# Attention scores: maximum pass that also copies to SBUF, whole-row exponentials, a one-pass difference, and 512-column projection products

## Chip, cores and metric

One core of a Trainium2 chip runs the whole program in one launch. The metric is device time in microseconds (us); the kernel before takes 5096.02 us, the median of 3 runs (5091.18 to 5097.48).

## What is computed

Two layers act on 2048 latent rows and 256 context rows of width 1024, all in float32. Layer one is an RWKV-7 mixer (input projection, two scans, readout and output product). Layer two, which the change is mostly about, is differential attention: 8 heads, each with two 64-wide query/key components and a 128-wide value.

```python
proj = h @ w_in                                   # q, k, v, g, 1024 columns each
s = jnp.einsum("bqhcd,bkhcd->bchqk", q_blk, k_all).astype(jnp.float32) * scale
p = jax.nn.softmax(s, axis=-1)                    # over 2304 keys, for c = 0 and 1
attn = p[:, 0] - lam * p[:, 1]
o = jnp.einsum("bhqk,bkhe->bqhe", attn, v_all)
y = rms_norm(o, subln) * (1.0 - lam_init)
x = x + gate * ((y * jax.nn.silu(g)) @ w_out)
```

## The kernel before

The stages follow each other: `phase1` (projection of layer one, from 0 to 1140 us in the profile), `phase2` (scans, to 2270), `readout` (to 2612), `project1` (layer two's projection, to 3398), `attention` (to 4870) and `finish` (output product). Float32 products are made of three products of split operands: a high part (float32r) and the rest, `matmul_split`, L928 to L933.

`readout` multiplies 18 blocks of 128 rows with the layer's output weights, four quarters of 256 columns each, and does norms on VectorE, ScalarE and GpSimd beside it; the string READ (L936) sets the order. `project1` goes over two groups of 1152 rows and eight chunks of 512 columns; each chunk's weights come as two tiles of 256 columns (`in_weights`, L1133), and a block of 128 rows takes 2 x 8 x 3 products of 256 columns (L1264 to L1266). The weights of the next chunk are asked for a third and two thirds of the way through a chunk (L1259).

`attention` goes over 8 heads with 16 query tiles of 128 rows each, 128 steps and two more that drain. The string STEP (L1294) sets one order for every engine, and `in_order` (L47) pins it on TensorE, VectorE, ScalarE and GpSimd: nothing overtakes. Step n does these for different tiles:

- C0, C1 (`scores`): for component c, five banks of 512 keys (the last has 256), two products each (L1403, L1404), and a VectorE maximum for each bank (L1405), then the maximum of the five (L1409). "@2T0a" means that transpose 0 comes after bank 2. The five PSUM banks are used by both components in turn.
- E0, E1 (`exponentials`): five ScalarE exponentials from PSUM with sums (L1418).
- J (`combine`, for tile n-1): sums, reciprocal and factor r (L1427 to L1430), then in three pieces of 768 columns VectorE multiplies P1 by r (L1433) and GpSimd adds it to P0 (L1434).
- T0 to T4, P0 to P4 (`values`, for tile n-2): transposes through two PSUM banks (tps), moved to SBUF by ScalarE or VectorE (L1451), and float32 products with the values (L1456, two instructions each); X copies the sum out (L1460).
- Q (`query`, for tile n+2): GpSimd doubles the query tile (L1349), TensorE flips it (L1354) into a tps bank, ScalarE copies it twice (L1384, L1385), and GpSimd forms the low part ql (L1386).
- K (`keys`, for the next head): in steps 4 to 14 of a head, blocks of 512 or 256 keys are doubled by GpSimd (L1349), flipped into a tps bank, and split by ScalarE (L1366) and VectorE (L1367). Ten steps of a head have a flip, in seven heads; we call them key steps.
- `readout1`: in the first steps of the next head, one small piece each step, on VectorE (L1474 to L1482, L70 to L79), then GpSimd products (L1486, L1487).

Of the kernel before, what the change touches and what calls it, by code (L numbers as in the profile page):

```python
# [23 lines left out]
T = NCTX + NLAT  # L24
# [914 lines left out]
def readout(k):  # L939

    nc, tc, S = k.nc, k.tc, k.S
    with ExitStack() as st:
# [6 lines left out]
        gp = pool("p3g", 2)  # L949
        wps = [pool(f"p3w{q}", 1) for q in range(4)]  # L950
        hp = pool("p3h", 2)
# [6 lines left out]
        gates = k.gates  # L958
        wH, wL = ([wps[q].tile([128, KT, 256], F32R, name=name) for q in range(4)] for name in ("woH", "woL"))

# [43 lines left out]
        def product(i, yH, yL):  # L1004
# [93 lines left out]
        with in_order(k, *engines):  # L1098
            for j in range(N + 1):
# [27 lines left out]
                if N > j >= N - 4 and j % 2 == 0:  # L1127
                    k.ahead.append(in_weights(k, k.early, len(k.ahead)))
# [4 lines left out]
def in_weights(k, pool, n):  # L1133

    wH = pool.tile([128, KT, 256], F32R, name="wH")
    wL = pool.tile([128, KT, 256], F32R, name="wL")
    cs = slice(256 * (n % 16), 256 * (n % 16) + 256)
    split_weights(k, k.raw, wH, wL, k.I["da_in"][0][:, cs])
    return wH, wL

# [25 lines left out]
def project1(k):  # L1166

    nc, tc, I, S = k.nc, k.tc, k.I, k.S
    with ExitStack() as st:
        pool = lambda name, bufs, **kw: st.enter_context(tc.tile_pool(name=name, bufs=bufs, **kw))  # L1170
        cp = pool("p4c", 1)
        hp = pool("p4h", 1)
        wp = pool("p4w", 2)
        rp = pool("p4t", 1)
# [15 lines left out]
        hL = hp.tile([128, KT, GRP], F32R, name="hL")  # L1190
        ready, count = k.ahead, itertools.count(len(k.ahead))

        def weights():
            n = next(count)
            if n < 16 * T // GRP:
                ready.append(in_weights(k, wp if n // 2 % 2 else k.early, n))

# [47 lines left out]
        for g in range(T // GRP):  # L1245
            for c in range(8):
                kind = "qqkkvvgg"[c]
                ws, ready[:] = list(ready), []
                pair = []
                skip = NCTX // 128 if g == 0 else 0  # L1250
                for at, i in enumerate((*range(skip, GT), *range(skip))):
# [38 lines left out]

CUT = (0, 768, 1536, T)


STEP = "C0@2T0a T1a J E0 P0 T2a J Q P1 C1@2T3a K5 S K4 P2 T4d J E1 P3 P4 Q Q X"  # L1294


def attention(k):

    nc, tc, I, S = k.nc, k.tc, k.I, k.S
    with ExitStack() as st:  # L1300
# [91 lines left out]
        def scores(n, c, between):  # L1392

            h, t = divmod(n, QTL)
            qh, ql = queries[n]
            cs = slice(128 * c, 128 * c + 128)
            mx = sp.tile([128, 5], F32, name=f"mx{c}")
            ps = []
            for b, (b0, b1) in enumerate(BANKS):
                s = sc.tile([128, 512], F32, name=f"sc{b}")  # L1400
                ps.append(s)
                ks = heads[h].ks[c][:, b0:b1]
                nc.tensor.matmul(s[:, :b1 - b0], qh[:, cs], ks, start=True, stop=False)  # L1403
                nc.tensor.matmul(s[:, :b1 - b0], ql[:, cs], ks, start=False, stop=True)  # L1404
                nc.vector.tensor_reduce(mx[:, b:b + 1], s[:, :b1 - b0], axis=AX.X, op=ALU.max)  # L1405
                if b in between:
                    between[b]()
            m = sp.tile([128, 1], F32, name=f"m{c}")
            nc.vector.tensor_reduce(m, mx, axis=AX.X, op=ALU.max, negate=True)  # L1409
            return ps, m  # L1410

        def exponentials(n, c, ps, m):
# [3 lines left out]
            z = sp.tile([128, 5], F32, name=f"z{c}")  # L1416
            for b, (b0, b1) in enumerate(BANKS):
                nc.scalar.activation(tiles[n][c][:, b0:b1], ps[b][:, :b1 - b0], AF.Exp, bias=m,  # L1418
                                     accum_out=z[:, b:b + 1])
            return z  # L1420

        def combine(n, z0, z1):

            h, t = divmod(n, QTL)
            zs = heads[h].z0[:, t:t + 1]
# [42 lines left out]
        def readout1(h, t0, t1):  # L1468
# [40 lines left out]
        with in_order(k, mybir.EngineType.PE, mybir.EngineType.DVE, mybir.EngineType.Activation, mybir.EngineType.Pool):  # L1509
            for n in range(N + 2):  # L1510
# [11 lines left out]
                def do(what):  # L1522
# [130 lines left out]
def block(tc, ins, out):  # L1653
    with ExitStack() as st:
# [7 lines left out]
        phase2(k)  # L1662
        with tc.tile_pool(name="early", bufs=2) as k.early, tc.tile_pool(name="gates", bufs=1) as gates, \
# [28 lines left out]
```

## Time and profile before

| | us |
|---|---|
| median of 3 runs | 5096.02 |
| the profiled execution: its own time | 5077.91 |
| its span | 5076.2 |
| TensorE busy | 4733.2 (93%) |
| VectorE busy | 3773.9 (74%) |
| ScalarE busy | 2866.3 (56%) |
| GpSimd busy | 2121.2 (42%) |

Busy times of a stage say more than those of the span, since each stage has its own limit. TensorE's matmuls are pipelined, so that a matmul's recorded length is longer than the distance to the next one; the distance is what counts where they run back to back.

### The profile page before, as it was taken

To read this page: it belongs to the slowest core of one execution; us is meant where nothing else is said; L and a number is where in the kernel's file an instruction comes from. 1 tells how busy PE (TensorE), PEld (TensorE's weight loads), DVE (VectorE), ACT (ScalarE), POOL (GpSimd) and SP (SyncE) were. 2 spreads that over 40 slices of the span, in tenths; PEclk is the share of its full clock that TensorE was granted. 3 is DMA by queue.
4 is the path that set the end of the run, shared out by engine and by line. 5 is a ranking of instruction groups with operands and counts; after the bars stand their busy time and mean duration, and the time that the engine had idled before them with its cause. 6 is when DMAs were issued, how large, how long until landed. Compare 5 with 4: busy or idle time off the path is not lost. (4 is left out here: it accounts for less than half of the span.)

```text
span 5076.2 us, 112658 instructions
## 1 busy us (share of the span) xinstructions
PE 4733.2 (93%) x44914; PEld 4416.5 (87%) x44914; DVE 3773.9 (74%) x6859; ACT 2866.3 (56%) x6810; POOL 2121.2 (42%) x2222
## 2 busy tenths in 40 slices
PE   7999999997989989887889999999999999999989
PEld 5999999995888888867789999988898888889887
DVE  6878777777777777758878258218889989989853
ACT  5565555554666666643331221118888888888830
POOL 1221112124555665523422022026677677767720
PEclk8999999998999999988999999999999999999999
DMA  4565565557666676676652332230110011010042
GB/s 169 164 185 174 175 178 163 172 160 202 160 169 159 162 171 169 174 246 190 202 161 91 110 105 86 94 110 1 28 45 25 21 45 35 27 28 18 10 154 91
DMA packets 624844, 612.86 MB, mean 121 GB/s; under 512 B 31622, under 2 KB 529721, under 8 KB 623297
## 3 DMA queue, kind: packets, MB, share of 16 engines
q1 hardware_dynamic: 621841, 601.99, 41.0%
q8 instruction: 355, 5.82, 0.5%
q10 hardware_dynamic: 2480, 3.67, 0.2%
q14 instruction: 168, 1.38, 0.1%
HBM read 405.79 MB, written 199.77 MB: 119 GB/s over the span
## 5 line engine op out<-in xcount | busy, mean ns | idle before, releaser
L1434 POOL TENSOR_TENSOR p<-p,p 128x768 f32<-128x768 f32 x384 | 730.4, 1916 | 347.1 <-DVE p L1433 340.5
L1418 ACT ACTIVATE p<-sc,m 128x512 f32<-128x512 f32 (+1 forms) x1280 | 805.7, 646 | 115.1 <-DVE m L1409 92.4
L1405 DVE TENSOR_REDUCE mx<-sc 128x1 f32<-128x512 f32 (+1 forms) x1280 | 732.8, 630 | 80.0 <-PE sc L1404 79.8
L932 PE MATMUL mmps<-wH,hH 128*128 128x256 f32 x2176 | 617.2, 284 | 3.3 <-ACT hH L91 3.1
L932 PE MATMUL mmps<-wL,hH 128*128 128x256 f32 x2176 | 616.9, 283 | 0.0
L932 PE MATMUL mmps<-wH,hL 128*128 128x256 f32 x2176 | 616.5, 283 | 0.0
L1456 PE MATMUL pv<-v,at 128*128 128x128 f32 x4608 | 610.8, 277 | 4.9 <-DVE at L1451 2.2
L1456 PEld LDWEIGHTS pv<-v,at 128*128 128x128 f32 x4608 | 559.7, 192 | 13.1 <-ACT at L1451 4.8
L1403 PE MATMUL sc<-ks,qh 128*128 128x512 f32 (+1 forms) x1280 | 529.6, 414 | 31.4 <-ACT p L1418 31.4
L1404 PE MATMUL sc<-ks,ql 128*128 128x512 f32 (+1 forms) x1280 | 467.3, 374 | 0.3 <-POOL ql L1386 0.3
L363 PE MATMUL mmps<-hH,wH 128*128 128x386 f32 x1632 | 429.3, 343 | 18.4 <-DVE sg L574 12.2
L363 PE MATMUL mmps<-hL,wH 128*128 128x386 f32 x1632 | 425.4, 341 | 2.1 <-DVE hL L92 2.1
L363 PE MATMUL mmps<-hH,wL 128*128 128x386 f32 x1632 | 424.9, 341 | 1.4 <-DVE nm_ss L197 1.2
L932 PEld LDWEIGHTS mmps<-wH,hH 128*128 128x128 f32 x2176 | 418.9, 192 | 4.0 <-ACT hH L91 4.0
L932 PEld LDWEIGHTS mmps<-wL,hH 128*128 128x128 f32 x2176 | 418.9, 193 | 0.0
L932 PEld LDWEIGHTS mmps<-wH,hL 128*128 128x128 f32 x2176 | 418.7, 192 | 0.0
L1449 PE MATMUL tps<-ident,p 128*128 128x128 f32 x2304 | 355.8, 272 | 0.0
L1403 PEld LDWEIGHTS sc<-ks,qh 128*128 128x128 f32 x1280 | 242.8, 190 | 105.3 <-ACT p L1418 70.8
L1451 ACT COPY at<-tps 128x512 f32<-128x512 f32 x512 | 292.7, 603 | 71.6 <-PE tps L1449 65.3
L363 PEld LDWEIGHTS mmps<-hH,wH 128*128 128x128 f32 x1632 | 296.7, 190 | 24.2 <-DVE sg L574 15.7
L1449 PEld LDWEIGHTS tps<-ident,p 128*128 128x128 f32 x2304 | 279.3, 141 | 33.6 <-issue 0.2
L363 PEld LDWEIGHTS mmps<-hH,wL 128*128 128x128 f32 x1632 | 300.4, 190 | 2.6 <-DVE nm_ss L197 2.0
(319 smaller groups left out, 11429.7 us busy)
## 6 DMA issues: line engine op xcount, KB each, us to landing
wr<-in_rw_in_dram SPq DMA_DIRECT2D x102, 512.0 KB
s_qr<-QR SPq DMA_DIRECT2D x48, 768.0 KB
BK<-s_bk SPq DMA_DIRECT2D x72, 512.0 KB
s_bk<-BK SPq DMA_DIRECT2D x47, 768.0 KB
wraw<-in_da_in_dram SPq DMA_DIRECT2D x64, 512.0 KB
BA<-s_bk SPq DMA_DIRECT2D x72, 256.0 KB
LA<-s_qr SPq DMA_DIRECT2D x72, 256.0 KB
BB<-s_bk SPq DMA_DIRECT2D x72, 256.0 KB
```

The source lines that it names most:

```text
L363: nc.tensor.matmul(a[:, :b1 - b0], wt[:, kt, :], ht[:, kt, b0:b1], start=(kt == 0 and wt is wH and ht is hH), stop=(kt == KT - 1 and last))
L932: k.nc.tensor.matmul(ps, s(kt), m(kt), start=(kt == 0 and s is sH and m is mH), stop=(kt == KT - 1 and last))
L1403: nc.tensor.matmul(s[:, :b1 - b0], qh[:, cs], ks, start=True, stop=False)
L1404: nc.tensor.matmul(s[:, :b1 - b0], ql[:, cs], ks, start=False, stop=True)
L1405: nc.vector.tensor_reduce(mx[:, b:b + 1], s[:, :b1 - b0], axis=AX.X, op=ALU.max)
L1418: nc.scalar.activation(tiles[n][c][:, b0:b1], ps[b][:, :b1 - b0], AF.Exp, bias=m, accum_out=z[:, b:b + 1])
L1434: nc.gpsimd.tensor_tensor(P0[:, b0:b1], P0[:, b0:b1], P1[:, b0:b1], op=ALU.add)
L1449: nc.tensor.transpose(ps[:, c - b0:c - b0 + 128], P0[:, c:c + 128], k.ident)
L1451: (eng.copy if eng is nc.scalar else eng.tensor_copy)(at[b][:, :b1 - b0], ps[:, :b1 - b0])
L1456: nc.tensor.matmul(acc, at[b][:, c - b0:c - b0 + 128], H.v[:, c // 128], start=(c == 0), stop=(c == T - 128))
```

## The change

It has four parts.

1. In `readout` and `project1` the weights lie in tiles of 512 columns, and one product writes 512 columns where two wrote 256.
2. In `scores` the banks form two groups, of 1024 and of 1280 keys. One VectorE instruction for each group negates the scores, writes them to the SBUF tile P, and gives their least value; the second group starts from the first's least value, so the last one is the row's. PSUM is free after that.
3. `exponentials` is one ScalarE instruction over 2304 columns, in place in SBUF, with the sum. The sums over five banks and the maximum of five fall away.
4. `combine` does P0 + r P1 in two VectorE instructions of 1152 columns (scalar_tensor_tensor); GpSimd's adds fall away. Transpose 4 is moved by ScalarE, all of `readout1`'s products go to GpSimd, and STEP is written anew.

```diff
@@ readout, products
-                    for q in range(2):
-                        w = 2 * half + q
-                        matmul_split(k, ps[:, 256 * q:256 * q + 256], lambda kt: yH[:, kt], lambda kt: yL[:, kt],
-                                     lambda kt: wH[w][:, kt], lambda kt: wL[w][:, kt])
+                    for k0 in range(0, KT, 4):
+                        matmul_split(k, ps, lambda kt: yH[:, kt], lambda kt: yL[:, kt], lambda kt: wH[half][:, kt],
+                                     lambda kt: wL[half][:, kt], k0, k0 + 4)
                         yield ps
...
@@ project1
-                    for half, (wH, wL) in enumerate(ws):
-                        matmul_split(k, ps[:, 256 * half:256 * half + 256], lambda kt: hH[:, kt, ts],
-                                     lambda kt: hL[:, kt, ts], lambda kt: wH[:, kt], lambda kt: wL[:, kt])
+                    matmul_split(k, ps, lambda kt: hH[:, kt, ts], lambda kt: hL[:, kt, ts], lambda kt: wH[:, kt],
+                                 lambda kt: wL[:, kt])
...
-CUT = (0, 768, 1536, T)
+CUT = (0, 1152, T)
+GROUP = (0, 1024, T)
-STEP = "C0@2T0a T1a J E0 P0 T2a J Q P1 C1@2T3a K5 S K4 P2 T4d J E1 P3 P4 Q Q X"
+STEP = "C0@0T0a+J T1a P0 J T2a E0 P1 Q C1@0T3a K5 K4 S P2 T4a P3 Q E1 P4 Q X"
...
@@ scores
+            for g, (g0, g1) in enumerate(zip(GROUP, GROUP[1:])):
+                s = sc.tile([128, -(-(g1 - g0) // 512) * 512], F32, name=f"sc{g}")
...
+                nc.vector.tensor_scalar(tiles[n][c][:, g0:g1], s[:, :g1 - g0], -1.0, m, op0=ALU.mult, op1=ALU.min,
+                                        accum_out=least)
+                m = least
...
@@ exponentials
-            for b, (b0, b1) in enumerate(BANKS):
-                nc.scalar.activation(tiles[n][c][:, b0:b1], ps[b][:, :b1 - b0], AF.Exp, bias=m,
-                                     accum_out=z[:, b:b + 1])
+            P = tiles[n][c]
+            nc.scalar.activation(P, P, AF.Exp, bias=m, scale=-1.0, accum_out=z)
...
@@ combine
-            nc.vector.tensor_reduce(r, z1, axis=AX.X, op=ALU.add)
-            nc.vector.tensor_reduce(zs, z0, axis=AX.X, op=ALU.add)
-            nc.vector.reciprocal(r, r)
-            nc.vector.scalar_tensor_tensor(r, r, neglam, zs, op0=ALU.mult, op1=ALU.mult)
+            nc.vector.reciprocal(r, z1)
+            nc.vector.scalar_tensor_tensor(r, r, neglam, z0, op0=ALU.mult, op1=ALU.mult)
...
-                nc.vector.tensor_scalar(P1[:, b0:b1], P1[:, b0:b1], r, None, op0=ALU.mult)
-                nc.gpsimd.tensor_tensor(P0[:, b0:b1], P0[:, b0:b1], P1[:, b0:b1], op=ALU.add)
+                nc.vector.scalar_tensor_tensor(P0[:, b0:b1], P1[:, b0:b1], r, P0[:, b0:b1], op0=ALU.mult, op1=ALU.add)
```

How the order moves is shown at three places of a key step. In the changed kernel the lines are L1405 and L1406 (score products), L1408 (the copy with the least value), L1419 (exponential), L1425 and L1426 (reciprocal, r), L1429 (difference), L1444 and L1446 (transpose and its copy), L1451 (value products) and L1455 (copy of their sum). A number after a name tells tiles of one name apart.

VectorE, around J, before (the last bank's maximum of C0 to the first of C1):

```order
L1405 TENSOR_REDUCE mx_41000<-sc_41024 128x1
L1409 TENSOR_REDUCE m_41028<-mx_41000 128x1
L1427 TENSOR_REDUCE r<-z_40977 128x1
L1428 TENSOR_REDUCE z_39147<-z_40900 128x1
L1429 RECIPROCAL r<-r 128x1
L1430 SCALAR_TENSOR_TENSOR r<-r,neglam,z_39147 128x1
L1433 TENSOR_SCALAR p_40899<-p_40899,r 128x768 x2
```

and in the change, from the last copy of a step on:

```order
L1408 TENSOR_SCALAR p_35875,m_35950<-sc_35943,m_35934 128x1280
L1367 TENSOR_TENSOR ks_35193<-tps,ks_35193 64x512
L1455 COPY o<-pv 128x128
L1408 TENSOR_SCALAR p_35991,m_35998<-sc_35993 128x1024
L1425 RECIPROCAL r<-z_35979 128x1
L1426 SCALAR_TENSOR_TENSOR r<-r,neglam,z_34975 128x1
L1429 SCALAR_TENSOR_TENSOR p_35874<-p_35875,r,p_35874 128x1152
L1408 TENSOR_SCALAR p_35991,m_36018<-sc_36011,m_35998 128x1280
L1429 SCALAR_TENSOR_TENSOR p_35874<-p_35875,r,p_35874 128x1152
```

The whole difference now stands on VectorE, its first half ahead of the second group's copy, on which the exponential waits.

GpSimd, one key step, before:

```order
L1349 TENSOR_TENSOR q_40045<-qraw,one 128x256
L1349 TENSOR_TENSOR k_40090<-kraw,one 128x512
L1434 TENSOR_TENSOR p_39878<-p_39878,p_39879 128x768
L1386 TENSOR_TENSOR ql<-qt,qh 128x256
L1434 TENSOR_TENSOR p_40024<-p_40024,p_40025 128x768 x2
```

and in the change:

```order
L1386 TENSOR_TENSOR ql<-qt,qh 128x256
L1349 TENSOR_TENSOR q_35693<-qraw,one 128x256
L1349 TENSOR_TENSOR k_35725<-kraw,one 128x512
L1386 TENSOR_TENSOR ql<-qt,qh 128x256
L1349 TENSOR_TENSOR q_35810<-qraw,one 128x256
```

With the adds gone, the two doublings of a step stand directly behind the ql of the step before, and wait for nothing in between.

TensorE in the change, from the flip of keys in a key step to the next step's first scores:

```order
L1354 MATMUL tps<-ident,k_36191 128x128 x4
L1451 MATMUL pv<-v,at 128x128 x4
L1444 MATMUL tps<-ident,p_35991 128x128 x2
L1451 MATMUL pv<-v,at 128x128 x4
L1354 MATMUL tps<-ident,q_36276 128x128 x2
L1451 MATMUL pv<-v,at 128x128 x2
L1405 MATMUL sc_36342<-ks_34971,qh 128x512
```

The flip of the query now stands ahead of the last value products (P4). As tps has two banks that are used in turn (keys, transpose 4, query), it writes the bank that the key block held.

## Rows read from the trace of the kernel before

**Rows 1.** Windows: us; busy (x) of PE, PEld, DVE, ACT, POOL; clock; DMA; three stages.

```profile
2270.00:2611.70 341.70, 269.32 (x2004) 262.25 (x2004) 285.77 (x423) 118.70 (x226) 124.81 (x69) 0.89 0.61 194
2611.70:3397.80 786.10, 785.92 (x6528) 785.63 (x6528) 391.06 (x804) 153.00 (x210) 127.94 (x99) 1.00 0.32 102
3439.50:4848.00 1408.50, 1377.18 (x9820) 1239.66 (x9821) 1266.14 (x2832) 1212.31 (x3595) 1013.80 (x755) 1.00 0.09 25
```

**Rows 2.** Chain of waits, one step without keys: start us, us, what.

```profile
3592.00 0.22 PE tps L1354 x2
3592.22 0.23 PE sc L1403
...
3599.99 0.89 PE pv L1456 x8
...
3602.44 0.22 PE tps L1354 x2
```

**Rows 3.** Timeline, VectorE: start us, us of the copy that ends a step.

```profile
3623.64 0.29 DVE L1460 COPY o<-pv 128x128 f32<-128x128 f32 x1 [0.32 <-PE pv L1456]
...
3684.78 0.28 DVE L1460 COPY o<-pv 128x128 f32<-128x128 f32 x1
...
3695.78 0.28 DVE L1460 COPY o<-pv 128x128 f32<-128x128 f32 x1
...
3803.63 0.29 DVE L1460 COPY o<-pv 128x128 f32<-128x128 f32 x1 [0.32 <-PE pv L1456]
```

**Rows 4.** Timeline, TensorE in finish: first and last of 43 products of 512 columns.

```profile
5001.96 0.39 PE L932 MATMUL mmps<-woH,yH 128*128 128x512 f32 x1
...
5011.51 0.39 PE L932 MATMUL mmps<-woH,yL 128*128 128x512 f32 x1
```

**Rows 5.** Groups by shape, VectorE: xcount | busy us, mean ns | idle before.

```profile
L1405 DVE TENSOR_REDUCE mx<-sc 128x1 f32<-128x512 f32 x1009 | 637.9, 684 | 72.8 <-PE sc L1404 72.7
L1405 DVE TENSOR_REDUCE mx<-sc 128x1 f32<-128x256 f32 x253 | 104.4, 413 | 0.0
L1367 DVE TENSOR_TENSOR ks<-tps,ks 64x512 fp32r<-64x512 f32 x56 | 38.9, 695 | 4.3 <-ACT ks L1366 0.5
L430 DVE SCALAR_TENSOR_TENSOR uk<-rm,vb,uk 128x768 f32<-128x768 f32 x24 | 24.2, 1010 | 0.0
```

**Rows 6.** Groups by shape, ScalarE and GpSimd.

```profile
L377 ACT ACTIVATE U<-U,omu 128x768 f32<-128x768 f32 x52 | 48.9, 941 | 46.9 <-POOL km L376 17.2 <-POOL rm L376 15.5 <-POOL vm L376 14.2
L377 ACT ACTIVATE U<-U,omu 128x512 f32<-128x512 f32 x26 | 18.8, 725 | 13.9 <-POOL km L376 5.8 <-POOL vm L376 4.9 <-POOL rm L376 3.1
L1386 POOL TENSOR_TENSOR ql<-qt,qh 128x256 fp32r<-128x256 f32 x125 | 91.6, 733 | 50.7 <-ACT qt L1385 45.5 <-issue 1.4 <-POOL p L1434 0.9
L1349 POOL TENSOR_TENSOR q<-qraw,one 128x256 f32<-128x256 f32 x125 | 77.9, 623 | 0.0
L1349 POOL TENSOR_TENSOR k<-kraw,one 128x512 f32<-128x512 f32 x56 | 62.2, 1110 | 0.0
```

**Rows 7.** Timeline, ScalarE: last exponential of a tile, its sum, a query copy.

```profile
3685.59 0.49 ACT L1418 ACTIVATE p<-sc,m 128x256 f32<-128x256 f32 x1
3685.95 0.23 ACT L1418 ACTIVATION_READ_ACCUMULATOR p<-sc,m 128x1 f32 x1
...
3686.29 0.42 ACT L1385 COPY qt<-tps 128x256 f32<-128x256 f32 x1
```

**Rows 8.** Timeline, VectorE: five maxima; then from the reciprocal to r's first use.

```profile
3592.72 2.84 DVE L1405 TENSOR_REDUCE mx<-sc 128x1 f32<-128x512 f32 x5 [0.39 <-PE sc L1404]
3595.85 0.16 DVE L1429 RECIPROCAL r<-r 128x1 f32<-128x1 f32 x1
...
3596.38 1.15 DVE L1433 TENSOR_SCALAR p<-p,r 128x768 f32<-128x768 f32 x2
```

**Rows 9.** Timeline: GpSimd, and VectorE beside it.

```profile
3659.77 1.85 POOL L1434 TENSOR_TENSOR p<-p,p 128x768 f32<-128x768 f32 x1 [0.49 <-PE tps L1354]
3659.81 1.83 DVE L72 TENSOR_TENSOR sub_t<-sub_y 128x16 f32<-128x16 f32 x1
```

More of the change, by code (lines that the diff above doesn't have):

```diff
@@ L949, in readout @@
         gp = pool("p3g", 2)
-        wps = [pool(f"p3w{q}", 1) for q in range(4)]
+        wps = [pool(f"p3w{half}", 1) for half in range(2)]
         hp = pool("p3h", 2)
@@ L958, in readout @@
         gates = k.gates
-        wH, wL = ([wps[q].tile([128, KT, 256], F32R, name=name) for q in range(4)] for name in ("woH", "woL"))
+        wH, wL = ([wps[half].tile([128, KT, 512], F32R, name=name) for half in range(2)] for name in ("woH", "woL"))
         def rows(i, first):
@@ L1127, in readout, with in_weights @@
                 if N > j >= N - 4 and j % 2 == 0:
-                    k.ahead.append(in_weights(k, k.early, len(k.ahead)))
+                    in_weights(k, k.early, k.ahead, (j - N + 4) // 2)
                 if N > j >= N - 3 and j % 2 == 1:
                     k.rows.append(in_rows(k, NCTX + 128 * len(k.rows)))
-def in_weights(k, pool, n):
-    wH = pool.tile([128, KT, 256], F32R, name="wH")
-    wL = pool.tile([128, KT, 256], F32R, name="wL")
+def in_weights(k, pool, ready, n):
+    if n % 2 == 0:
+        ready.append([pool.tile([128, KT, 512], F32R, name=name) for name in ("wH", "wL")])
+    wH, wL = (t[:, :, 256 * (n % 2):256 * (n % 2) + 256] for t in ready[-1])
     cs = slice(256 * (n % 16), 256 * (n % 16) + 256)
     split_weights(k, k.raw, wH, wL, k.I["da_in"][0][:, cs])
-    return wH, wL
 def in_rows(k, t0):
@@ L1172, in project1 @@
         hp = pool("p4h", 1)
-        wp = pool("p4w", 2)
+        wp = pool("p4w", 1)
         rp = pool("p4t", 1)
@@ L1190, in project1 @@
         hL = hp.tile([128, KT, GRP], F32R, name="hL")
-        ready, count = k.ahead, itertools.count(len(k.ahead))
+        ready, count = k.ahead, itertools.count(2 * len(k.ahead))
         def weights():
@@ L1195, in weights @@
             if n < 16 * T // GRP:
-                ready.append(in_weights(k, wp if n // 2 % 2 else k.early, n))
+                in_weights(k, wp if n // 2 % 2 else k.early, ready, n)
         def store(c, t0, out):
@@ L1247, in project1 @@
                 kind = "qqkkvvgg"[c]
-                ws, ready[:] = list(ready), []
+                wH, wL = ready.pop()
                 pair = []
@@ L1396, in scores @@
             cs = slice(128 * c, 128 * c + 128)
-            mx = sp.tile([128, 5], F32, name=f"mx{c}")
-            ps = []
-            for b, (b0, b1) in enumerate(BANKS):
[L1400 to L1412, printed above, removed]
             if c == 0:
                 tiles[n] = [pp.tile([128, T], F32, name="p0", bufs=3), pp.tile([128, T], F32, name="p1")]
-            z = sp.tile([128, 5], F32, name=f"z{c}")
-            for b, (b0, b1) in enumerate(BANKS):
-                nc.scalar.activation(tiles[n][c][:, b0:b1], ps[b][:, :b1 - b0], AF.Exp, bias=m,
-                                     accum_out=z[:, b:b + 1])
+            m = None
@@ new lines, in scores @@
+            for g, (g0, g1) in enumerate(zip(GROUP, GROUP[1:])):
+                s = sc.tile([128, -(-(g1 - g0) // 512) * 512], F32, name=f"sc{g}")
+                for b0 in range(g0, g1, 512):
+                    b1 = min(b0 + 512, g1)
+                    ks = heads[h].ks[c][:, b0:b1]
+                    nc.tensor.matmul(s[:, b0 - g0:b1 - g0], qh[:, cs], ks, start=True, stop=False)
+                    nc.tensor.matmul(s[:, b0 - g0:b1 - g0], ql[:, cs], ks, start=False, stop=True)
+                least = sp.tile([128, 1], F32, name=f"m{c}{g}")
+                nc.vector.tensor_scalar(tiles[n][c][:, g0:g1], s[:, :g1 - g0], -1.0, m, op0=ALU.mult, op1=ALU.min,
+                                        accum_out=least)
+                m = least
+                if g in between:
+                    between[g]()
@@ L1420, in exponentials @@
+            return m
+        def exponentials(n, c, m):
+            z = heads[n // QTL].z0[:, n % QTL:n % QTL + 1] if c == 0 else sp.tile([128, 1], F32, name="z1")
+            P = tiles[n][c]
+            nc.scalar.activation(P, P, AF.Exp, bias=m, scale=-1.0, accum_out=z)
             return z
         def combine(n, z0, z1):
-            h, t = divmod(n, QTL)
-            zs = heads[h].z0[:, t:t + 1]
             r = sp.tile([128, 1], F32, name="r")
-            nc.vector.tensor_reduce(r, z1, axis=AX.X, op=ALU.add)
@@ L1484, in readout1 @@
                 cs = slice(c, c + (4 if t0 == 0 else 2))
-                eng = nc.gpsimd if c % 4 == 0 else nc.vector
+                eng = nc.gpsimd
                 eng.tensor_tensor(H.o[:, cs], H.o[:, cs], H.sg[:, cs], op=ALU.mult)
@@ L1538, in do @@
                         if n < N:
-                            z = exponentials(n, int(arg), *state[arg])
+                            z = exponentials(n, int(arg), state[arg])
                             zs.setdefault(n, []).append(z)
@@ L1662, in block @@
         phase2(k)
-        with tc.tile_pool(name="early", bufs=2) as k.early, tc.tile_pool(name="gates", bufs=1) as gates, \
+        with tc.tile_pool(name="early", bufs=1) as k.early, tc.tile_pool(name="gates", bufs=1) as gates, \
                 tc.tile_pool(name="raw", bufs=2) as k.raw:
```

3 lines of the change are left out of this document (2 added, 1 removed).

## Prediction

> **What bounds the kernel now.** I read the busy times by stage first [rows 1]: TensorE is busy 785.92 of project1's 786.10 us and 1377 of 1408.5 us (98%) of steady attention, so there its work is the time. In readout it is busy 269 and VectorE 286 of 342 us; neither fills the stage. VectorE has 90% of attention, so a change that gives it work can move the bound there.
>
> Then the chain of waits for a step of attention without keys [rows 2]: from one flip of the query to the next (3592.00 to 3602.44) every link is TensorE's, 10.44 us. VectorE's timeline [rows 3] gives the other steps by the copy that ends each: a key step takes 3695.78 - 3684.78 = 11.0 (the flip of four key blocks adds four of the two-block flip's 0.11, so 10.88, and a little wait), and a whole head with keys and readout pieces 3803.63 - 3623.64 = 180.0. Ten steps of 11.0 and six of 10.44 are 172.6; the other 7.4 go to the readout pieces. [rows 9] show how: a VectorE operation of 16 columns, where one of a single column takes 0.16 [rows 8], lasts 1.83 us beside a GpSimd add of 1.85, and ends with it.
>
> **The 512-column products.** In project1 6528 products of 256 columns fill 785.92 us [rows 1]: 0.2408 a pair. One product of 512 columns for such a pair stands in finish [rows 4]: 43 of them start from 5001.96 to 5011.51, 9.55 / 42 = 0.2274 apart. 3264 x 0.0134 = **43.8 us less**. Weights are asked for at the same points of a chunk and TensorE waits for none of them now, so a chunk that needs both halves at its start costs nothing; if one half came late, the loss would show as a gap between chunks. Readout has 864 pairs: 11.6 us if TensorE bounded it, 0 if the norms do; TensorE has 79% and VectorE 84% of the stage, and I take 5.
>
> **Attention, prices of the new instructions.**
> - Copy with least value, from PSUM. The maxima [rows 5] take 684 ns for 512 columns and 413 for 256: 1.06 ns a column, so 1.23 us for 1024 and 1.50 for 1280. Five in a row take 2.84 [rows 8] where the sum is 3.15: 0.08 overlap each.
> - Fetching the least value has no row on VectorE. Below: 0. Above: ScalarE's fetch of a sum, 0.23 [rows 7], which there delays the next instruction by 0.09 only (3685.95 to 3686.04). I take 0.09 in the queue. Where the second copy needs the first's least value I add a wait of 0.2, as from the reciprocal's start to that of what needs it (3595.85 to 3596.05, before r's use at 3596.38).
> - Difference, 1152 columns: 1.010 for 768 [rows 5] and 384 x 1.06 ns: 1.42, in the queue 1.34.
> - Exponential of 2304 columns: 0.941 for 768, and 0.725 for 512 [rows 6], so 0.844 ns a column: 2.24.
>
> What goes away on VectorE is ten maxima (8 x 0.684 + 2 x 0.413 = 6.3 us) and the pieces of J; on GpSimd three adds of 1.85. Transpose 4's copy goes to ScalarE, which has 14% of attention free [rows 1] and loses ten exponentials for two; that costs nothing, and a longer queue there would show ahead of the exponential. All readout products on GpSimd run under the 5.5 us that the adds leave.
>
> **Attention, steps without keys.** On VectorE, from the end of a step's last copy: E1 follows and r can be had after 2.24 + 0.04 + 0.53 (reciprocal to r's use [rows 8]), 2.8. Then first half of the difference 1.34, second copy 1.50 - 0.08 + 0.09 = 1.51, second half 1.34, C1's copies 1.24, wait 0.2, and 1.59: 7.22. Together 10.0, under TensorE's 10.44. These stay TensorE's: 10.5.
>
> **Key steps.** Two paths lead from the last copy to the first difference.
> - Through TensorE. The query's flip now stands ahead of P4 and writes the bank from which L1367 reads the keys; L1367 stands behind the last copy. So: L1367 0.70 [rows 5], flip 0.22 and P4 0.45 (four of eight in 0.89) and four score products of 0.23 [rows 2], the last product's tail 0.16 (0.39 recorded, 0.2274 apart [rows 4]), three hand-overs of 0.04: 2.57. Copy 1.24: 3.81. Reciprocal and r 0.53: **4.34**.
> - Through GpSimd. The exponential ends its queue share 2.11 after its start (2.24 less the 0.13 by which the fetch overlaps [rows 7]), and the query's two copies are done 0.76 after that (3685.95 to 3686.71 [rows 7]): with hand-overs 2.95. Then ql 0.73 and two doublings 0.62 and 1.11 [rows 6] follow without a wait: to 5.41. A two-input VectorE operation that comes while a GpSimd one runs is held until its end, less about 0.15 [rows 9]. The doubling of keys starts at 4.30, 0.04 ahead of the difference: start at **5.26**.
>
> So the ring is 5.26 + 7.22 = 12.48, and 11.98 for the two key blocks of 256 (a doubling 0.5 shorter). A head with both is 8 x 12.48 + 2 x 11.98 + 6 x 10.5 + 2 for readout pieces (7.4 now, mostly behind adds that are gone) = 188.8, against 180.0: +8.8, six heads, +53. The first head has no readout pieces: 186.8 against 172.6, +14. The last has no keys: 170 against 175, -5. The 70 key steps thus move from TensorE's bound to a ring through all four engines. Attention **+62**.
>
> Sum on the profiled execution: 5077.9 + 62 - 43.8 - 5 = 5091. The median is 18.1 above that execution, and I carry it: **5109 us**.
>
> The Trainium skill ("SBUF — State Buffer", section "SBUF: two separate sides") says that VectorE and GpSimd share a port pair as an exclusive lock for a whole instruction, and that a VectorE operation with two SBUF inputs takes part against a GpSimd one that reads SBUF. [...]
>
> **Rivals.**
> - *The difference meets no doubling* (faster). It decides at 4.30: if VectorE comes 0.04 us earlier than I have it, or the doublings have run before, the difference goes first and GpSimd waits behind it. The ring is 4.34 + 7.22 = 11.56: 56 x 0.92 + 14 x 0.42 = 57 us less, **5052**. If the fetch is free as well, 4 x 0.09 x 70 = 25 less, 5027. For it: 0.04 us is less than I can place; against: three GpSimd operations in a row leave little room.
> - *The fetch of the least value is dear*: 0.23 where I have 0.09. Four copies stand in the ring: 0.56 x 70 = 39, and steps without keys come to 10.6, 0.13 x 58 = 8: **5156**. For it: the one row of a fetch [rows 7] lasts as long; against: on ScalarE it overlaps.
> - *The difference runs at half rate*: 1152 x 1.06 ns more, 1.22 each. Key steps +2.44 x 70 = 171, the others 10.07 + 2.44 - 10.5 = 2.0 x 58 = 117: **5397**. Against: L430, of the same form, does 768 columns in 1.010 [rows 5], 1.3 ns a column with all its fixed cost. The Trainium skill ("Vector Engine (DVE) Microarchitecture Reference", section "7. Points that are easy to get wrong") says that such an instruction with two SBUF sources that are not bf16 has half the throughput; L430 is float32 and does not show it against 1.06 ns from one source.
> - *The change does not do what it says*: the order of instructions has every step where the change's words put it, so I give it no chance of its own.
>
> **How the numbers follow.** Forecast 0.45, with a range of its own of 5084 (fetch free, -25) to 5132 (fetch halfway to 0.23, +23). No doubling met 0.36, dear fetch 0.16, half rate 0.03. From 5027 (the first rival at its best) to 5165 (the second, and 9 for the readout gain of 5 and of the pieces that may fail to come) the range leaves out half rate, the tails of the two, and little else. Within 0.2%, some 10 us, no difference could be told: 5086 to 5106. The forecast's range puts 0.02 below, 0.18 in and 0.25 above it; the first rival lies below, the others above: faster 0.38, same 0.18, slower 0.44.
>
> **What would show it.** Project1 at about 742 us, its products 0.227 apart. In attention, key steps of about 12.4 and the others of 10.5; the difference L1429 with a mean above 1.42 and, ahead of it or within it, the doublings of L1349 just ended; TensorE's idle time ahead of L1405 (scores) and the query's flip, ended by VectorE. If key steps take 11.5 and L1429 has 1.4, the first rival holds; a fetch row of 0.2 or more between L1408 and the next instruction means the second; L1429 at 2.6 in every step the third. The prediction is wrong at its root if steps without keys take over 11 us, since then VectorE's prices are off, or if project1 keeps 786.

## The result and the profile after

The changed kernel takes 5019.59 us, the median of 4 runs (5011.7 to 5029.73), against 5096.75 for the kernel before in the same comparison: a ratio of 0.9861, with a 95% interval from 0.9846 to 0.9877, so 1.4% faster. The prediction was 5109, with a range from 5027 to 5165: wrong in the direction, and just outside the range. In a later comparison (below) the ratio was 0.9877, from 0.9853 to 0.9901.

| us | before | after |
|---|---|---|
| median | 5096.75 | 5019.59 |
| the profiled execution: its own time | 5077.91 | 5014.9 |
| its span | 5076.2 | 5013.2 |
| TensorE busy | 4733.2 | 4677.5 (93%) |
| VectorE busy | 3773.9 | 3764.6 (75%) |
| ScalarE busy | 2866.3 | 2678.0 (53%) |
| GpSimd busy | 2121.2 | 1510.5 (30%) |

Windows of the changed kernel's profile, the columns as in [rows 1]: readout, project1, and attention without its two ends.

```profile
2270.00:2610.40 340.40, 265.43 (x1139) 219.07 (x1138) 286.37 (x421) 116.91 (x224) 124.99 (x69) 0.86 0.60 192
2610.40:3352.60 742.20, 742.18 (x3263) 614.30 (x3264) 394.50 (x806) 153.85 (x211) 127.70 (x99) 1.00 0.34 108
3392.00:4790.00 1398.00, 1371.39 (x9831) 1240.66 (x9829) 1256.57 (x1830) 1029.03 (x1707) 412.15 (x376) 1.00 0.09 26
```

Project1 takes 742.2 us where it took 786.1 [rows 1]: 43.9 less. Readout ends 1.3 us earlier and no more; 0.9 of that was there before its first product (2268.9 against 2269.8).

The copies of a sum, of before and of after: count, ns of one (least, median, most), start of the first and the last.

```profile
L1460 DVE COPY o<-pv x128: 276/292/295, 3451.9 to 4863.3; 128x128 f32<-128x128 f32 x128
L1455 DVE COPY o<-pv x128: 290/291/294, 3403.7 to 4802.4; 128x128 f32<-128x128 f32 x128
```

From the first copy to the last, attention took 1411.4 us and now takes 1398.7: 12.7 less. Its filling is 3.0 shorter and what follows the last copy 2.1. Together 43.9 + 1.3 + 12.7 + 3.0 + 2.1 = 63.0, the difference of the two profiled executions. The medians differ by 77, since the execution of before that was profiled lay 19 us under its median, and the one of after 5. In the later comparison they differ by 58 (5092.12 and 5033.79). The 63, which stands on stages, is the firmer figure.

Groups by shape on VectorE in attention, and one line of the page for ScalarE; columns as in [rows 5].

```profile
L1429 DVE SCALAR_TENSOR_TENSOR p<-p,r,p 128x1152 f32<-128x1152 f32 x256 | 426.9, 1668 | 4.5
L1408 DVE TENSOR_SCALAR_CACHE_REDUCE p<-sc,m 128x1280 f32<-128x1280 f32 x256 | 395.5, 1545 | 18.1 <-PE sc L1406 1.6 <-DVE p L1408 0.5 <-PE tps L1444 0.5
L1408 DVE TENSOR_SCALAR_CACHE_REDUCE p<-sc 128x1024 f32<-128x1024 f32 x256 | 311.5, 1217 | 56.7 <-PE sc L1406 55.6
L1426 DVE SCALAR_TENSOR_TENSOR r<-r,neglam,z 128x1 f32<-128x1 f32 x128 | 50.9, 397 | 4.5
...
L1408 DVE DVE_READ_ACCUMULATOR p<-sc,m 128x1 f32 x256 | 20.6, 80 | 0.0
```

```profile
L1419 ACT ACTIVATE p<-p,m 128x2304 f32<-128x2304 f32 x256 | 568.8, 2222 | 201.0 <-DVE p L1408 198.4
```

Almost every price of the prediction stands here: copies of 1.22 and 1.55 us (1.23 and 1.50 said), a fetch of the least value of 0.08 (0.09), an exponential of 2.22 (2.24). The difference has a mean of 1.668, over the 1.42 of one that nothing holds.

### The profile page after: what moved, and what is told of

The parts are those of the page before. It is cut to its first block, busy times and chain, and to the rows that moved or that the text cites. A ratio compares the mean times of both kernels' runs of the same rounds, so it can differ in the third digit from the quotient of the medians.

```text
span 5013.2 us, 101038 instructions
## 1 busy us (share of the span) xinstructions
PE 4677.5 (93%) x40786; PEld 4202.4 (84%) x40786; DVE 3764.6 (75%) x5833; ACT 2678.0 (53%) x4890; POOL 1510.5 (30%) x1840
## 4 chain that ended last, share of the span: by engine, by line
PE 36%; DVE 6%; issue 5%; ACT 2%; POOL 1%; DMA 0%; POOLq 0%; ACTq 0%; DVEq 0%; SPq 0%
PE mmps L932 16%; PE pv L1451 8%; PE tps L1444 4%; PE sc L1405 3%; PE sc L1406 3%; DVE p L1408 3%; DVE p L1429 2%; PE tps L1354 1%; DVE r L1426 1%; ACT at L1446 1%; ACT p L1419 1%; POOL out L1279 0%; PE tps L1594 0%; ACT ht L220 0%; ACT qt L1385 0%
## 5 line engine op out<-in xcount | busy, mean ns | idle before, releaser
L1419 ACT ACTIVATE p<-p,m 128x2304 f32<-128x2304 f32 x256 | 568.8, 2222 | 201.0 <-DVE p L1408 198.4
L1451 PE MATMUL pv<-v,at 128*128 128x128 f32 x4608 | 626.4, 277 | 6.3 <-ACT at L1446 4.4
L1451 PEld LDWEIGHTS pv<-v,at 128*128 128x128 f32 x4608 | 564.4, 192 | 16.2 <-ACT at L1446 12.9
L1405 PE MATMUL sc<-ks,qh 128*128 128x512 f32 (+1 forms) x1280 | 520.6, 407 | 15.3 <-DVE p L1408 15.2
L1406 PE MATMUL sc<-ks,ql 128*128 128x512 f32 (+1 forms) x1280 | 464.0, 372 | 0.3 <-POOL ql L1386 0.3
L1446 ACT COPY at<-tps 128x512 f32<-128x512 f32 (+1 forms) x640 | 345.2, 540 | 179.4 <-PE tps L1444 175.5
L1429 DVE SCALAR_TENSOR_TENSOR p<-p,r,p 128x1152 f32<-128x1152 f32 x256 | 426.9, 1668 | 4.5
L932 PE MATMUL mmps<-wH,hH 128*128 128x512 f32 x1088 | 424.8, 390 | 3.1 <-ACT hH L91 3.1
L932 PE MATMUL mmps<-wL,hH 128*128 128x512 f32 x1088 | 424.5, 390 | 0.0
L932 PE MATMUL mmps<-wH,hL 128*128 128x512 f32 x1088 | 424.0, 390 | 0.0
L1408 DVE TENSOR_SCALAR_CACHE_REDUCE p<-sc,m 128x1280 f32<-128x1280 f32 x256 | 395.5, 1545 | 18.1 <-PE sc L1406 1.6
L1444 PE MATMUL tps<-ident,p 128*128 128x128 f32 x2304 | 361.6, 275 | 10.3 <-ACT qt L1385 5.4
L1408 DVE TENSOR_SCALAR_CACHE_REDUCE p<-sc 128x1024 f32<-128x1024 f32 x256 | 311.5, 1217 | 56.7 <-PE sc L1406 55.6
L1444 PEld LDWEIGHTS tps<-ident,p 128*128 128x128 f32 x2304 | 273.2, 141 | 60.8 <-ACT at L1446 11.2
L363 PEld LDWEIGHTS mmps<-hL,wH 128*128 128x128 f32 x1632 | 301.4, 191 | 3.3 <-DVE hL L92 3.3
L700 POOL TENSOR_TENSOR N<-N,rank 128x30 f32<-128x30 f32 (+14 forms) x510 | 278.8, 547 | 40.0
```

The costliest lines, as they stand in the source:

```text
L363: nc.tensor.matmul(a[:, :b1 - b0], wt[:, kt, :], ht[:, kt, b0:b1], start=(kt == 0 and wt is wH and ht is hH), stop=(kt == KT - 1 and last))
L700: eng.tensor_tensor(N[:, m + 1:32, 0:m], N[:, m + 1:32, 0:m], t, op=ALU.subtract)
L932: k.nc.tensor.matmul(ps, s(kt), m(kt), start=(kt == 0 and s is sH and m is mH), stop=(kt == KT - 1 and last))
L1405: nc.tensor.matmul(s[:, b0 - g0:b1 - g0], qh[:, cs], ks, start=True, stop=False)
L1406: nc.tensor.matmul(s[:, b0 - g0:b1 - g0], ql[:, cs], ks, start=False, stop=True)
L1408: nc.vector.tensor_scalar(tiles[n][c][:, g0:g1], s[:, :g1 - g0], -1.0, m, op0=ALU.mult, op1=ALU.min, accum_out=least)
```

## Where the key steps went

The forecast hung on one thing, key steps of 12.48 us. The distances of the copies of a sum show what they are: in the first head 10.8 to 11.1; in the second to seventh seven of ten are 10.8 to 11.1 (one in all 11.27) and three are 12.36 to 12.66; steps without keys take 10.5 to 10.9 (one 11.1). A head takes 178.2 to 178.6 where it took 179.7 to 181.0, the first 174.6 where it took 171.7.

Timeline of the changed kernel, one key step of the first head: the end of a step, and what leads to the first difference of the next. Columns: start us, us, engine, line and instruction.

```profile
3466.52 1.55 DVE L1408 TENSOR_SCALAR_CACHE_REDUCE p<-sc,m 128x1280 f32<-128x1280 f32 x1
...
3467.95 0.38 PE L1354 MATMUL tps<-ident,q 128*128 128x128 f32 x2
3468.11 0.69 DVE L1367 TENSOR_TENSOR ks<-tps,ks 64x512 fp32r<-64x512 f32 x1
...
3468.54 0.47 PE L1405 MATMUL sc<-ks,qh 128*128 128x512 f32 x1
3468.83 0.29 DVE L1455 COPY o<-pv 128x128 f32<-128x128 f32 x1
3469.74 1.22 DVE L1408 TENSOR_SCALAR_CACHE_REDUCE p<-sc 128x1024 f32<-128x1024 f32 x1 [0.61 <-PE sc L1406]
...
3471.03 0.73 POOL L1386 TENSOR_TENSOR ql<-qt,qh 128x256 fp32r<-128x256 f32 x1 [8.11 <-ACT qt L1385]
3471.20 0.57 DVE L1426 SCALAR_TENSOR_TENSOR r<-r,neglam,z 128x1 f32<-128x1 f32 x1
3471.72 0.61 POOL L1349 TENSOR_TENSOR q<-qraw,one 128x256 f32<-128x256 f32 x1
3471.81 1.74 DVE L1429 SCALAR_TENSOR_TENSOR p<-p,r,p 128x1152 f32<-128x1152 f32 x1
...
3472.29 2.15 POOL L1349 TENSOR_TENSOR k<-kraw,one 128x512 f32<-128x512 f32 x1
```

The flip of the query starts at 3467.95, before L1367 does (3468.11). It did not wait for it. The sentence ahead of the prediction that this flip writes the bank that the key block held is wrong: in the built program, in all 70 key steps, the key block's tile has bank 5, transpose 4 bank 6, the query bank 6 again, and transpose 0 of the next step bank 5. The pool does not give its two banks in turn. The listing of the built program shows it by the waits (Activation is ScalarE, Pool GpSimd, DVE VectorE): the query's flip waits for ScalarE (and the doubling), not for VectorE; it is transpose 0 that waits for VectorE, for L1367, and that stands behind the first group's scores.

```text
L1354 MATMUL tps_38297<-ident_74,q2_38248 128x128 [waits Activation_49,Pool_49]
L1405 MATMUL sc0_38314<-ks0_35193,qh_38188 128x512 [waits DVE_49]
L1444 MATMUL tps_38321<-ident_74,p0_38078 128x128 [waits DVE_49]
```

So L1367's 0.70 leaves the path through TensorE. The last copy ends at 3468.07 and the first difference starts at 3471.81, 3.74 later; the prediction's 4.34 less 0.70 is 3.64. ql starts 2.96 after it (3471.03), where the prediction had 2.95. So the difference comes 0.48 us ahead of the doubling of keys. It meets only the query's doubling (1.74 instead of 1.42), and the doubling of keys takes 2.15 us, held until the difference ends.

The theory that I then tested: only that wait was wrong, prices and hold were right. The rival: the ring was priced too high elsewhere too.

## Experiments

**The wait put in.** A copy of one column of the doubled query, on VectorE behind L1367, makes the flip wait as the prediction had it (`key_step` holds in steps 5 to 14 of a head that has a next one; lines after the edit are up by 3).

```diff
@@ query
+            if n >= 2 and key_step(n - 2):
+                nc.vector.tensor_copy(q2[:, 0, 0, 0:1], q2[:, 0, 0, 0:1])
             ps = tp.tile([128, 512], F32, name="tps")
             flip(ps, q2)
```

> The changed kernel, with one thing added in each of the 70 key steps: a VectorE copy of one column of the doubled query, behind the subtraction of the keys (L1367), so that the flip of the query waits for that subtraction, as the prediction had it. Theory: the prediction failed in that one step. In the changed kernel the flip got the PSUM bank that transpose 4 had left, which ScalarE reads, and did not wait for VectorE; the prices and the hold by GpSimd were right. Then key steps now rise from 10.8 to 11.1 us to the forecast's ring: 11.6 if the difference still gets ahead of the doubling of keys, up to 12.5 if not; the total rises by 40 to 110 us, to 5060 to 5130. Rival: the ring was priced too high in other places (VectorE has slack to hide the wait); then key steps stay within 0.15 us of now, and the total within 10 us of 5020.

It took 5094.5 us (median of 10; before 5091.44; ratio 1.0016, from 1.0000 to 1.0032): the whole gain was gone, since attention now took 1465.8 us from first to last copy, 54 more than before the change (62 in the prediction) and 67 more than the changed kernel. The usual key step of the first head is 12.36 us (12.48 in the prediction), the first head 184.8 (186.8), the next six 187.8 (188.8). The copies of a sum, and the timeline of one step:

```profile
L1458 DVE COPY o<-pv x128: 291/292/293, 3411.9 to 4877.7; 128x128 f32<-128x128 f32 x128
```

```profile
3478.07 1.55 DVE L1411 TENSOR_SCALAR_CACHE_REDUCE p<-sc,m 128x1280 f32<-128x1280 f32 x1
...
3479.66 0.69 DVE L1367 TENSOR_TENSOR ks<-tps,ks 64x512 fp32r<-64x512 f32 x1
...
3480.39 0.15 DVE L1380 COPY q<-q 128x1 f32<-128x1 f32 x1
3480.69 0.41 PE L1354 MATMUL tps<-ident,q 128*128 128x128 f32 x2 [0.91 <-DVE q L1380]
...
3483.27 0.62 POOL L1349 TENSOR_TENSOR q<-qraw,one 128x256 f32<-128x256 f32 x1
...
3483.85 1.04 POOL L1349 TENSOR_TENSOR k<-kraw,one 128x512 f32<-128x512 f32 x1
3483.86 1.05 DVE L1429 SCALAR_TENSOR_TENSOR r<-r,neglam,z 128x1 f32<-128x1 f32 x1
...
3484.94 1.42 DVE L1432 SCALAR_TENSOR_TENSOR p<-p,r,p 128x1152 f32<-128x1152 f32 x1
```

The last copy ends at 3479.62 and the difference (L1432) starts at 3484.94, 5.32 later, where the prediction had 5.26. What the doubling of keys held was the little product for r (L1429, one column, 1.05 us instead of 0.22), and the difference behind it. The added copy itself lengthens the path to the flip by 0.3 us (3480.39 to 3480.69), and r starts only 0.01 behind the doubling of keys. One step of the first head shows that this does not decide: there L1367 has half a block (0.43 us), so that all behind it comes 0.26 earlier.

```profile
3495.95 0.32 DVE L1429 SCALAR_TENSOR_TENSOR r<-r,neglam,z 128x1 f32<-128x1 f32 x1
3496.21 1.04 POOL L1349 TENSOR_TENSOR k<-kraw,one 128x512 f32<-128x512 f32 x1
3496.30 2.16 DVE L1432 SCALAR_TENSOR_TENSOR p<-p,r,p 128x1152 f32<-128x1152 f32 x1
```

Here r gets ahead of the doubling of keys. The last copy ended at 3491.98; the doubling starts 4.23 later (4.30 in the prediction) and the difference 4.32 (4.34), so the difference itself is held, to 2.16, and the step takes 12.38. The theory holds and the rival falls: with the wait, the key steps are those of the forecast within some 0.1 us. No run has the copy without the wait; the copy by itself takes 0.15.

**The wait put in, and GpSimd's work moved away.** Both additions of the runs e1 and e7 (below) at once: the first rival of the prediction as it was written.

> Both additions at once: the flip of the query waits for the keys' subtraction, and GpSimd's work stands behind the second difference. It is the prediction's first rival as it was written: the difference meets no doubling, on the ring through TensorE. Theory: key steps of 11.5 to 11.6 (4.34 and 7.22, worked out as 11.56 there) where no product or piece is beside them, as in the first head, against 12.36 with the doublings ahead. Rival: the price of the hold was wrong, and key steps stay at 12.2 or more, or fall below 11.2.

One execution, 5056.42 us. Seven of the first head's ten key steps take 11.52 to 11.54 us (two with half a block 11.26 and 11.27, the very first 12.10); 11.56 was the price of that rival.

```profile
3485.29 1.55 DVE L1411 TENSOR_SCALAR_CACHE_REDUCE p<-sc,m 128x1280 f32<-128x1280 f32 x1
...
3488.80 0.29 DVE L1458 COPY o<-pv 128x128 f32<-128x128 f32 x1 [1.04 <-PE pv L1454]
...
3491.33 1.42 DVE L1432 SCALAR_TENSOR_TENSOR p<-p,r,p 128x1152 f32<-128x1152 f32 x1
...
3495.63 0.19 POOL L1546 TENSOR_TENSOR gate<-p,one 128x1 f32<-128x1 f32 x1 [5.09 <-DVE p L1432]
3495.77 0.62 POOL L1349 TENSOR_TENSOR q<-qraw,one 128x256 f32<-128x256 f32 x1
```

The difference starts 4.49 after the last copy's end (3486.84), 4.34 and the added copy's 0.15, and takes 1.42. From its start to the end of the ring there are 11.53 - 4.49 = 7.04, and in e1 12.36 - 5.32 = 7.04, where the prediction had 7.22; that 11.53 lies so near 11.56 is in part luck, as the copy's 0.15 makes up for this. The hold by GpSimd cost 12.36 - 11.53 = 0.83 a key step in e1. The wait for L1367 with the added copy costs the rest: e7, the same kernel without them, has 10.82 in these steps, and 1385.6 us from first to last copy against 1425.4 here.

**The two halves of the change apart.** The 512-column products with the old attention, and the new attention with the old products.

> The 512-column products of readout and project1 alone, with the attention of before. Theory: project1 takes 742 us and readout loses 1 to 2, since its norms bound it, so 44 to 46 us less than before: some 5051, and attention as before (1411 us from the first copy of a sum to the last). Rival: readout gains 5 or more as predicted, or the shorter project1 moves something in attention: 50 us less or more, or under 40.

It took 5040.14 (ratio 0.9909, from 0.9890 to 0.9928), 51 less; project1 742 us, first to last copy of attention 1413.6. By the medians it is 5 more than the theory said, and past the 50 of the rival. The stages speak for the theory: 44 in project1, 0.5 in readout (341.5 us from its first product to project1's, where before has 342.0), and attention 2 longer than before. The rest lies within the spread told of below.

> The attention of the changed kernel alone, with the 256-column products of before. Theory: 13 us less between the first and the last copy of a sum and some 3 at the two ends, so 16 less than before by the profiles, and not over 32 by the medians: 5065 to 5080. By the prediction's own sum for attention it would be 62 more: 5159. Rival: attention is worth nothing by itself (within 5 us of before), and its gain in the changed kernel hangs on the projection's.

It took 5072.47 (ratio 0.9967, from 0.9952 to 0.9983), 19 less, and 1398.6 us from first to last copy, the changed kernel's 1398.7. The halves add up (51 + 19 = 70, where the whole gave 77 and in the later comparison 58) and do not need each other: each keeps its stage's time without the other.

**GpSimd's work behind the difference.** One GpSimd product of one column reads the last column of the difference, and everything behind it in GpSimd's queue waits.

```diff
-STEP = "C0@0T0a+J T1a P0 J T2a E0 P1 Q C1@0T3a K5 K4 S P2 T4a P3 Q E1 P4 Q X"
+STEP = "C0@0T0a+J T1a P0 Jh R T2a E0 P1 Q C1@0T3a K5 K4 S P2 T4a P3 Q E1 P4 Q X"
...
+                        if arg == "h" and 1 <= n <= N:
+                            gate = sp.tile([128, 1], F32, name="gate")
+                            nc.gpsimd.tensor_tensor(gate, tiles[n - 1][0][:, T - 1:T], one, op=ALU.mult)
...
```

> The changed kernel, with GpSimd's work moved away from the difference: a GpSimd product of one column that reads the last column of the difference stands ahead of the readout products and of the doublings of query and keys, so that these start when the second difference is done; the readout's pieces are issued there too. Theory: the three steps of 12.4 to 12.7 us in each head from the second to the seventh are the difference held by GpSimd products; the stretched L1429 (mean 1.668, 1.42 alone) is the doublings. Then L1429 has a mean of 1.42 to 1.47, no step of these heads is over 11.3, a head takes 172 to 174 instead of 178.2, and the total falls by 25 to 45 us, to 4975 to 4995. Rival: the work moved is late for the flips or holds VectorE's copies in its new place, steps stay at 11.3 or more, and the total is within 10 us of 5020 or above.

Half of it came. The three long steps are gone, L1429 has a mean of 1.439, and a head takes 175.6 to 176.1; first to last copy 1385.6 us, 13 less. But the first steps of a head rose to 11.0 to 11.8, since R (which issues the readout's pieces there) set their small VectorE operations ahead of C1's copies, and the steps with neither keys nor pieces to 10.8. The median, 5018.5, is that of the changed kernel, as the rival had it and not 25 to 45 less: the profiled run reached project1 at 2632.9 us, 22 later than the changed kernel's did (see the last section), so that the gain shows in attention alone.

The long steps themselves, in the changed kernel: one of 12.64, from the copy that ends the step before to its own.

```profile
3621.38 0.29 DVE L1455 COPY o<-pv 128x128 f32<-128x128 f32 x1
...
3623.64 0.68 DVE L1426 SCALAR_TENSOR_TENSOR r<-r,neglam,z 128x1 f32<-128x1 f32 x1
3624.26 1.27 POOL L1481 TENSOR_TENSOR o<-o,sg 128x512 f32<-128x512 f32 x1
3624.36 2.40 DVE L1429 SCALAR_TENSOR_TENSOR p<-p,r,p 128x1152 f32<-128x1152 f32 x1
...
3625.62 2.04 POOL L1482 TENSOR_TENSOR o<-o,sub_y 128x512 f32<-128x512 f32 x1
...
3628.15 2.29 DVE L1429 SCALAR_TENSOR_TENSOR p<-p,r,p 128x1152 f32<-128x1152 f32 x1
3628.19 1.04 POOL L1349 TENSOR_TENSOR k<-kraw,one 128x512 f32<-128x512 f32 x1
...
3634.02 0.29 DVE L1455 COPY o<-pv 128x128 f32<-128x128 f32 x1
```

A readout product (L1481) that starts 0.10 ahead of the difference holds it to 2.40 us; the doublings that were pushed back then hold the second half to 2.29.

**The same in key steps alone**, with the small pieces left at the step's end (lines of `attention` are up by 1).

```diff
-STEP = "C0@0T0a+J T1a P0 J T2a E0 P1 Q C1@0T3a K5 K4 S P2 T4a P3 Q E1 P4 Q X"
+STEP = "C0@0T0a+J T1a P0 J G T2a E0 P1 Q C1@0T3a K5 K4 S P2 T4a P3 Q E1 P4 Q X"
...
+                    elif kind == "G":
+                        if key_step(n):
+                            gate = sp.tile([128, 1], F32, name="gate")
+                            nc.gpsimd.tensor_tensor(gate, tiles[n - 1][0][:, T - 1:T], one, op=ALU.mult)
+                            if t >= 6:
+                                next(rgen, None)
...
-                for _ in range(2 if n > N - 4 else 1):
+                for _ in range(2 if n > N - 4 else 0 if key_step(n) and t >= 6 else 1):
```

> The changed kernel with GpSimd's products and doublings behind the second difference in key steps alone; the readout's small VectorE pieces stay at the step's end, and steps without keys stay as they are. Theory: what spoiled half of the gain when all was moved were those small pieces, which then stood ahead of C1's copies on VectorE (first steps of a head 11.2 to 11.8 us), and the steps without keys (10.78 instead of 10.55). Then steps without keys take 10.5 to 10.6, key steps 10.8, those with products 11.1: heads two to seven 173 to 175.5 us instead of 178.2, 1375 to 1384 between first and last copy of a sum (1398.7 now, 1385.6 with all moved), and the total 15 to 24 us below the changed kernel's of the same call. Rival: the later doublings themselves cost (keys or query late for their flips), and the steady stretch stays at 1386 or more.

> The changed kernel once more, on the chip of the run it is compared with. Theory: steady attention 1398 to 1399 us again, while the start of project1 moves by up to 30 us from run to run, with the clock granted before it; the median within 10 us of 5020.

It took 4997.84 us (median of 5), and the changed kernel in the same comparison 5033.79 (of 6, and 14 above the 5020 expected): 36 less. Against before the ratios are 0.9812 (0.9788 to 0.9835) and 0.9877 (0.9853 to 0.9901), which do not overlap. Heads two to seven take 174.1 to 174.4 us, key steps 10.8 and those with products 11.1; first to last copy 1371.7 us, under the 1375 to 1384 expected and 27.0 less than the changed kernel's 1398.7, which came again. The medians' 36 is more than the 15 to 24 expected and than the stage's 27; in the profiled executions the other 9 stand before project1 (2620.7 against 2630.1). It is the fastest kernel of this study. Its copies of a sum, and the timeline of a step with products:

```profile
L1456 DVE COPY o<-pv x128: 291/292/294, 3413.8 to 4785.5; 128x128 f32<-128x128 f32 x128
```

```profile
3643.59 1.42 DVE L1430 SCALAR_TENSOR_TENSOR p<-p,r,p 128x1152 f32<-128x1152 f32 x1
...
3646.39 1.42 DVE L1430 SCALAR_TENSOR_TENSOR p<-p,r,p 128x1152 f32<-128x1152 f32 x1
...
3647.72 1.22 DVE L1409 TENSOR_SCALAR_CACHE_REDUCE p<-sc 128x1024 f32<-128x1024 f32 x1
3647.89 0.19 POOL L1550 TENSOR_TENSOR gate<-p,one 128x1 f32<-128x1 f32 x1 [4.70 <-DVE p L1430]
...
3648.03 1.28 POOL L1482 TENSOR_TENSOR o<-o,sg 128x512 f32<-128x512 f32 x1
...
3649.08 1.55 DVE L1409 TENSOR_SCALAR_CACHE_REDUCE p<-sc,m 128x1280 f32<-128x1280 f32 x1
...
3649.39 1.04 POOL L1483 TENSOR_TENSOR o<-o,sub_y 128x512 f32<-128x512 f32 x1
```

In this step the products, beside the copies from PSUM (L1409), take 1.28 and 1.04 us and the copies 1.22 and 1.55: neither holds the other.

**Products shared again**, a miss.

> The changed kernel with every second pair of readout products on VectorE again, as before the change (four pieces in each head, two on each engine). Theory: the steps of 12.4 to 12.7 us stand beside GpSimd's products; there are then one or two of them in a head instead of three, and the steps with VectorE's products take 1.2 to 1.5 us more than 10.9, since VectorE has little left: 176.5 to 178.5 a head, no change of the total by more than 10 us. Rival: GpSimd's products are not the cause, and the same three steps stay long.

One execution, 5035.15 us, 1398.9 from first to last copy, the same three long steps. It says nothing about the cause: in seven heads the pieces go over four tiles at a time, and the condition that chose VectorE held for none of them, before the change as well. The edit moved one piece in the last head's tail. That part of the change, which the prediction took for a move of work, is nearly empty.

## Why the prediction was wrong, and where it was right

- **Right: the 512-column products.** 43.8 us said for project1, 43.9 measured.
- **Too much: readout.** 5 said, within 0 to 11.6; it ended 1.3 earlier, with TensorE's busy time 4 us less (265 against 269, at a granted clock of 0.86 against 0.89) and VectorE's the same 286. That the norms' chain sets it fits these rows, but no run tested it.
- **Right: the prices** of copy, fetch, exponential and difference; with them fall the rivals of a dear fetch (0.080 us, where that rival had 0.23) and of half rate (1.42, where it had 2.6). The difference takes 1.42 where nothing holds it; from L430's 1.010 for 768 columns [rows 5] that is 1.07 ns a column more, the slope of the maxima, which read PSUM. The Trainium skill ("Vector Engine (DVE) Microarchitecture Reference", section "7. Points that are easy to get wrong") says half throughput. The trace agrees if the measure is one input from SBUF: L1433 of the kernel before, float32 too, took 0.62 for 768 columns (rows in the last section). The prediction compared with the maxima, and so saw no halving; its price was right, since L430, from which it came, has two SBUF inputs itself.
- **Wrong: the step "The query's flip now stands ahead of P4 and writes the bank from which L1367 reads the keys".** It writes the bank of transpose 4, so that nothing on the path waits for L1367. The first difference starts 3.74 after the last copy, where the forecast had 5.26. With the 7.04 that follow its start (shown by e1 and e5, 7.22 said) the ring is 10.78, and 11.10 with the 0.32 by which the query's doubling holds the difference: the 11.1 of the first head. Where nothing holds it (e7, e8) key steps take 10.82, near the 10.88 that the prediction had for TensorE. In e1, with the wait, the difference starts at 5.32 and the ring is 12.36, where the forecast had 5.26 and 12.48.
- **The first rival's mechanism came, and more.** The difference does go ahead of the doubling of keys, but with 0.48 us to spare where 0.04 was to decide, and the ring it was priced with (11.56, shown by e5 as 11.53) was also the one with the wait. Hence 5019.6 and not 5052. That this lies only 7 us outside the range is luck: the range's lower end, 5027, is this rival with the wait and with a fetch that costs nothing, and neither is what came.
- **Right in kind, not seen in place: the hold by GpSimd.** The prediction let all readout products run under time that the adds leave, at no cost. They stand behind ql, just ahead of the difference, and make three steps of a head 12.36 to 12.66: 1.5 to 1.8 us each above 10.9, in six heads some 30 us. e8 takes back 25 in these heads, and 2 in the first, where only the doublings hold. The Trainium skill's exclusive lock ("SBUF — State Buffer", section "SBUF: two separate sides") agrees, in both directions: 2.40 and 2.15 us. Whether it is a port, the runs cannot say; they show it only as times.
- **Attention as a whole**: +62 said. First head 174.6 and not 186.8, the next six 178.3 on the mean and not 188.8, the last 5 less as said: 12 + 63 = 75 us away from the forecast. By the profiled executions the miss is 5091 - 5015 = 76, so this is nearly all of it (readout 4 worse than said and the two ends 5 better make up the rest). By the medians it is 89, since the forecast carried 18 us from the profiled execution of before to the median, and after has 5.

## What to carry to other kernels

A path that rests on which buffer a tile gets has to be read from the built program's waits, not from the number of buffers and an order in turn: here the wait that was read wrongly is worth 67 us of attention (e1 against the changed kernel). Where VectorE's two-input operations and GpSimd share a stretch, look for what stands just ahead of them in GpSimd's queue, and move GpSimd's work beside VectorE's reads of PSUM; a one-column product as a gate does that in a hand-written order. Small operations that a rearrangement puts ahead of a copy on a busy engine can give back part of what it gains, as in e7.

## What the runs showed that I had not expected

- A one-column operation is held like a large one: r took 1.05 us behind a doubling of keys, 0.22 alone.
- A product of one SBUF tile is cheaper by the column than the difference, and was held by GpSimd too. Two such lines of the kernel before: count, ns of one (least, median, most), start of the first and the last.

```profile
L1433 DVE TENSOR_SCALAR p<-p,r x384: 606/619/1446, 3435.1 to 4855.8; 128x768 f32<-128x768 f32 x192
L199 DVE TENSOR_SCALAR x<-x,nm_y x18: 750/753/755, 15.6 to 603.7; 128x1024 f32<-128x1024 f32 x18
```

By the medians that is 0.52 ns for each column more, half of the difference's 1.07. 68 of the 384 took over 0.7 us, up to 1.446, and each of these started beside a GpSimd operation. So the difference was not the first instruction of this stage to meet GpSimd.

- The time before layer two moves from run to run by more than most effects studied here: project1 started between 2606.6 us (e2) and 2640.9 (e3), though nothing before readout differs and readout by 1.4 us. In a window of phase2 the granted clock was lower in the later one. Windows of e2 and of e3, columns as in [rows 1]:

```profile
1140.00:2240.00 1100.00, 972.94 (x19037) 878.29 (x19038) 837.25 (x1187) 678.55 (x1588) 607.09 (x1093) 0.95 0.70 177
```

```profile
1140.00:2240.00 1100.00, 974.69 (x18406) 885.82 (x18406) 827.18 (x1177) 663.01 (x1559) 600.11 (x1092) 0.91 0.67 170
```

In the same 1100 us TensorE did 18406 products at a clock of 0.91 and 19037 at 0.95. What lowers it was not tried. Attention, at a granted clock of 1.00 in these runs, repeats far better: 1398.7, 1398.6 and 1398.7 us for the changed one, 1411.4 and 1413.6 for the one of before. So single stages tell parts of a change apart that medians of a few runs do not.
